# Queries, keys, features and B turned by transposing DMA reads instead of TensorE, with SyncE's reads in a fixed order

## The chip, the cores and the metric

The kernel runs on one core of one Trainium2 chip. The metric is the device time in microseconds (us) of one execution of the whole layer; lower is better. All engines of the core (TensorE, VectorE, ScalarE, GpSimd, SyncE) run beside each other and meet at semaphores. In the profile they are PE (with PEld, its weight loads), DVE, ACT, POOL and SP; a `q` behind the name means that the engine's queue waits or issues.

## The reference, cut to what matters

One layer of a decoder on 256 tokens of width 2048, all in float32:

```python
h = h + 0.5 * swiglu(rmsnorm(h, ffn1_norm), ffn1_w_gu, ffn1_w_down)          # d_ff 5632
proj = rmsnorm(h, mix_norm) @ w_in                                           # u, v, z, x, B, C, dt
a_out = chunked_sgu(gelu(u), gelu(v), gm_v_norm, gm_w_s, gm_b_s)
m_out = mamba2_group(z, xbc, dt, ...)     # conv + silu on x/B/C, chunked scan, D skip, silu(z) gate, norm
h = h + concat([a_out, m_out]) @ w_out
h = h + memory_cross_attention(rmsnorm(h, xa_norm), rmsnorm(mem, mem_norm), w_q, w_kv, w_o)  # 4 heads of 512
h = h + 0.5 * swiglu(rmsnorm(h, ffn2_norm), ffn2_w_gu, ffn2_w_down)
return rmsnorm(h, final_norm)
```

In the attention, `logits = q k^T / sqrt(512)` per head over 256 memory tokens, then a softmax, then `probs @ v` and `w_o`. The scan uses x, B and C after their convolution, with x and B needed with tokens on the partitions.

## The kernel before, in words

**Pieces of weights.** Every projection reads its weights from DRAM in pieces, mostly 1 MB into one of three `raw` buffers (`load`, line 136). ScalarE casts a piece to `hi` (line 169), VectorE subtracts to get `lo` (line 177), and TensorE multiplies the activations with both (`matmul`, line 74): products high x high, high x low and low x high. Some pieces are of kind "S", in which sums of blocks save one of eight products; the others are "C". `proj_tok`, `proj_feat` and `proj_sum` are the three shapes of a projection. A normal piece is 24 matmuls of 512 columns.

**The order of the work.** TensorE's instructions stay in program order. All others are placed by a scheduler that orders each engine's instructions when the kernel is built, unless `behind(...)` (tc.issue_after) ties one behind another. Work that belongs to an earlier stage is put off with `later(fn, by)`: `step()` counts pieces (or halves of them) and runs what is due. `by=2` therefore means "two pieces from here". Jobs that need a PSUM bank are held back while the eight banks are in use; those marked `bankless` are not.

**Activations have to be turned.** A product needs its activations with the contracted dimension on the partitions. There are two ways in this kernel. `to_operand` with a list transposes on TensorE (line 77, tile `tpose`, four 128x128 instructions for half of an operand) and splits from PSUM. `turn_over` goes through DRAM: ScalarE copies a float tile into two 16-bit halves (`halves`, line 369), GpSimd's queue writes them (`planes`, line 371), SyncE's queue reads them back with a transposing DMA (`turned`, line 375), and the split takes them from SBUF. `by=(a, b)` gives the pieces until the first read and from each read until the split. The hidden operands of both feed-forward blocks, the first two chunks of the mix operand (`xt_mix`) and the gated operand `at` are turned by DMA; the queries and keys (`qt`, `kt`, from `part` tiles), the convolved features x (`xf`, evacuated into `y` at line 854) and B (`bt`) are turned on TensorE.

**Buffers.** Temporaries share six buffers (`half_k`, tag `t2k`): halves, turned operands, partial sums (`part`), gates and others. Twelve large slots hold operands, `y`, the scan's tiles and values. SyncE's queue holds the weight reads and the transposing reads.

**Stages around the change.** After the first feed-forward block: B and C (`proj_feat`), x (`proj_feat`), V, U and Z (`proj_tok`) with the scan's steps in between (`scan_start`, `scan_decay`, `scan_apply`; `xdt` is the product of the features and dt at line 875), then `w_out`, the queries, keys, values, `w_o`, and the second feed-forward block. `attend` makes the logits of a head from `qts` and `kts`.

Of the kernel before, what the change touches and what calls it, by code (L numbers as in the profile page):

```python
# [17 lines left out]
P = 128  # L18
# [16 lines left out]
KG = 4  # L35
# [12 lines left out]
def hybrid_layer(ctx: ExitStack, tc: tile.TileContext, x, xt, mem, memt, w_gu1, w_dn1, w_in, w_s, w_out,  # L48
# [84 lines left out]
    PLAIN = {(0, 0): 0, (0, 1): 1, (1, 0): 2, (1, 1): 3}  # L133
    FOR_SUMS = {(0, 0): 0, (1, 0): 1, (1, 1): 2, (0, 1): 3}

    def load(w, r0, cs, at, fine=False):
        raw = wraw.tile([P, 2 * KP, NC], F32, name="raw")
        rows = w[r0:r0 + KP * P, :]
        if at is PLAIN and cs[1] == cs[0] + NC:
            nc.sync.dma_start(out=raw.rearrange("p (k j) n -> p k j n", j=2), in_=rows[:, cs[0]:cs[0] + 2 * NC].rearrange(  # L140
                "(k p) (j n) -> p k j n", p=P, j=2))
            return raw
        if fine:
            for (k, j), b in at.items():
                nc.sync.dma_start(out=raw[:, b, :], in_=rows[k * P:(k + 1) * P, cs[j]:cs[j] + NC])
            return raw
        for j, c in enumerate(cs):
            b, e = at[0, j], at[1, j]
            src = rows[:, c:c + NC]
            if e > b:  # L150
                nc.sync.dma_start(out=raw[:, b:e + 1:e - b, :], in_=src.rearrange("(k p) n -> p k n", p=P))
                continue
            for k, x in enumerate((b, e)):
                nc.sync.dma_start(out=raw[:, x, :], in_=src[k * P:(k + 1) * P, :])
        return raw

    def behind(instructions):

        order = ExitStack()
        for ins in instructions:  # L160
            order.enter_context(tc.issue_after(ins))
        return order

    last_cast = []

# [158 lines left out]
    def proj_feat(w, xts, n0):  # L324
        ps = {}
        n = D // P // (2 * KP)
        for i in range(n):
            raw = wraw.tile([P, 2 * KP, NC], F32, name="raw")
            nc.sync.dma_start(out=raw, in_=w[2 * i * KP * P:2 * (i + 1) * KP * P, n0:n0 + NC].rearrange(
                "(k p) n -> p k n", p=P))  # L330
            hi, lo = split(raw)
            order = [(k, c) for k in range(2 * KP) for c in range(4)]
            if i in (0, n - 1):
                order.sort(key=lambda kc: kc[1])
            for a in range(0, len(order), 4):
                for w_part in (hi, lo):
                    for k, c in order[a:a + 4]:
                        kt = 2 * i * KP + k
                        if c not in ps:
                            ps[c] = side("acc")  # L340
                        xt = xts[kt // KG][:, kt % KG, :]
                        w_kc = w_part[:, k, c * P:(c + 1) * P]
                        if w_part is hi:
                            matmul(ps[c], w_kc, xt, start=kt == 0)
                        else:
                            matmul(ps[c][:, S:], w_kc, xt[:, :S], stop=kt == D // P - 1)
            step()
        return [ps[c] for c in range(4)]
# [22 lines left out]
            nc.gpsimd.dma_start(out=planes[t * P:(t + 1) * P].rearrange("p b n -> p (b n)"), in_=halves)  # L371
        return planes

    def read_turned(to, planes, c0, n):
        nc.sync.dma_start(out=to, in_=planes[:, :, c0:c0 + n].rearrange("s b n -> (s b) n"), transpose=True)

    def turn_over(srcs, by, put):
        planes = write_planes(srcs)

        def fetch(q):  # L380
            to = half_k(F32, "turned")
            read_turned(to.bitcast(U16).rearrange("p (k s) -> p k s", k=KP), planes, q * P, KP * P)
            later(lambda: put(to.rearrange("p (k s) -> p k s", k=KP), q), by=by[1], bankless=True)

        for q in (0, 2):
            later(lambda q=q: fetch(q), by=by[0] + q / 4, bankless=True)

    def in_turn(src, last, op, c0=None):

# [66 lines left out]
    class Pieces(dict):  # L456
# [59 lines left out]
                                             op=ALU.subtract)  # L516
            return hi.ins, lo.ins

        def turn_later(self, srcs, by, c0=None, at=None):
            if at is None:  # L520
                at = self.due
                self.due += 2
            turn_over(srcs, by, lambda to, q: self.put(at + q // 2, to, q, c0))

        def later(self, srcs, c0=None, by=1):
            for q in (0, 2):
# [2 lines left out]
    class Normed:  # L529
# [8 lines left out]
        def chunk(self, n, by=1):  # L538
            srcs = [h[n][:, t, :] for t in range(NT)]
            if n < 2 and not isinstance(self.xts, Pieces):  # L540
                operand_turned(srcs, self.xts, f"xt_{self.name}{n}", self.c0 + n * KG, (2.5 + 1.5 * n, 2.5))
                self.stats(n)
            elif isinstance(self.xts, Pieces):

                for i in (2 * n, 2 * n + 1):
                    later(lambda i=i: self.xts.put(i, srcs, i % 2 * KP, self.c0 + n * KG),
                          self.bys.get(i, by))
                later(lambda: self.stats(n), self.stats_by)
            else:
                operand_later(srcs, self.xts, f"xt_{self.name}{n}", self.c0 + n * KG, by)  # L550
                self.stats(n)
# [59 lines left out]
    def ffn(nrm, w_gu, w_dn, done=None, each=None, fine=0, by_token=False):  # L611
        for c_from, c_to in ((0, 5), (5, 11)):
            kinds, turn = DN_KINDS[c_to - c_from]
            hts = Pieces(kinds, "hid", nrm.xts)
            for c in range(c_from, c_to):
                m = {}
                gs = []

                def mid(banks):
                    m["m1"], m["y"], m["z"], m["y2"] = parts_of(banks)  # L620

                def evac(t, j, ps):
                    g, u = (m["z"], m["y2"]) if t else (m["m1"], m["y"])
                    if j == 0:
                        total(g, ps, g, ALU.subtract if t else ALU.add)
                        nc.scalar.activation(g, g, AF.Silu, scale=nrm.rstd[:, t:t + 1])
                        return
                    total(u, ps, u)
                    nc.vector.scalar_tensor_tensor(out=g, in0=u, scalar=nrm.rstd[:, t:t + 1], in1=g,
                                                   op0=ALU.mult, op1=ALU.mult)  # L630
                    gs.append(g)

                if c == 0:
                    proj_sum(w_gu, 0, nrm.xts, FIRST_KINDS, (c * NC, DFF + c * NC), mid, evac, FIRST, fine)
                else:
                    proj_sum(w_gu, 0, nrm.xts, GU_KINDS, (c * NC, DFF + c * NC), mid, evac, GU_ORDER)
                hts.turn_later(gs, (1, 4))
            last = c_to == 11
            add_sum(w_dn, c_from * NC, hts, (kinds, kinds), turn, 0.5, done if last else None, each if last else None,
                    last and by_token)  # L640

# [186 lines left out]
    bt = slot([P, GROUPS, S], F32, "bt")  # L828
    ctr = slot([P, GROUPS, S], F32, "ct")
    def b_tokens(q):  # L830
        ps = side("tpose")
        for i in range(4):
            transpose(out=ps[:, i * P:(i + 1) * P], in_=bt[:, q * 4 + i, :P], identity=ident)
        nc.any.tensor_copy(out=btok[:, q * 4:q * 4 + 4, :], in_=ps.rearrange("p (g n) -> p g n", n=P))

    for c in range(4):
        xis = gather(proj_feat(w_in, nx.xts, B0 + c * NC))
# [3 lines left out]
        for i in range(4):  # L841
            conv_silu(xis[i], 16 + c * 4 + i, dst[:, (c % 2) * 4 + i, :])
        if c < 2:
            later(lambda c=c: b_tokens(c), by=2)
    y = [slot([P, HEADS, HD], F32, f"y{t}") for t in range(NT)]

    def x_tokens(c, i0, xf):
        tps = side("tpose").rearrange("p (t k s) -> p t k s", t=NT, k=2)
        for t in range(NT):
            for i in range(2):  # L850
                transpose(out=tps[:, t, i, :], in_=xf[:, i, t * P:(t + 1) * P], identity=ident)
        for t in range(NT):
            h0 = (c * 4 + i0) * 2
            nc.any.tensor_copy(out=y[t][:, h0:h0 + 4, :],
                               in_=tps[:, t].rearrange("p k (h d) -> p (k h) d", d=HD))

    for c in range(4):
        xis = gather(proj_feat(w_in, nx.xts, X0 + c * NC))
        for i0 in (0, 2):
            xf = half_k(F32, "xf").rearrange("p (k s) -> p k s", k=2)  # L860
            for i in range(2):
                conv_silu(xis[i0 + i], c * 4 + i0 + i, xf[:, i, :])
            later(lambda c=c, i0=i0, xf=xf: x_tokens(c, i0, xf), by=2 + i0 // 2)


    def per_head(ap, n):
# [5 lines left out]
    def scan_start(t, j):  # L872
        if j == 0:
            scan["xdt"] = scan[f"xdt{t}"] = xdt = slot([P, HEADS, HD], F32, "xdt")
            nc.vector.tensor_tensor(out=xdt, in0=y[t], in1=per_head(dt[:, t, :], HD), op=ALU.mult)
            nc.vector.tensor_tensor(out=y[t], in0=y[t], in1=per_head(rowb[:, 2, :], HD), op=ALU.mult)
        dec = slot([P, 16, P], F32, "dec")
        nc.gpsimd.dma_start(
# [60 lines left out]
                            base=0, channel_multiplier=-1)  # L939
    v = [slot([P, 4, NC], F32, f"v{t}") for t in range(NT)]  # L940
    ss_v = small.tile([P, NT, 4], F32, name="ss_v", bufs=1)
    for i, (by, to) in enumerate(((3, 8), (8, 12), (14, 18.5), (18.5, 23))):
        later(lambda i=i: scan_start(i // 2, i % 2), by=by)
        later(lambda i=i: scan_apply(i // 2, i % 2), by=to)
    for c in (0, 2):
# [31 lines left out]
    for c in (0, 2):  # L977
# [10 lines left out]

        proj_tok(w_in, 0, nx.xts, (U0 + c * NC, U0 + (c + 1) * NC), evac)
        for j in range(2):  # L990
            ats.turn_later(gss[j], (2.5 + 1.5 * j, 2.5))

    ss_m = small.tile([P, NT, 4], F32, name="ss_m", bufs=1)
    for c in (0, 2):
# [71 lines left out]
    def by_head(to, name, scale=None):  # L1066
        got = {}

        def take(j, t, x):
# [1 line left out]
            if scale is not None:  # L1071
                nc.scalar.mul(x, x, scale[:, t:t + 1])
            if t == 1:
                operand_later([got[j, 0], got[j, 1]], to, name, by=1 + j / 2)

        return take

# [40 lines left out]
    for hd in (0, 2):  # L1118
        heads(w_kv, mem_ts, MEM_KINDS, MEM_ORDER, hd * XD, by_head(kts, "kt", rstd_mem))
        for j in range(2):  # L1120
            later(lambda hd=hd + j: attend(hd, kts[hd]), by=2 + j / 2)

    O_KINDS = "CCCSCSCC"
    ots = Pieces(O_KINDS, "ot")
# [100 lines left out]
```

## Time and profile before

| what | value |
|---|---|
| median of 3 runs | 2428.43 us (2428.28 to 2432.98) |
| profiled execution | 2428.32 us |
| its span, first to last instruction | 2426.6 us |
| granted TensorE clock | 0.999 |
| PE / DVE / ACT / POOL busy | 2413.6 / 2033.3 / 1361.4 / 65.4 us |
| HBM read / written | 476.76 / 16.81 MB |

The busy time of an engine is summed over its instructions without overlaps, and its share is of the span. The profile lists groups of instructions by line and by tiles, written as out<-in, with the idle time of the engine just ahead of them and what ended it; the chain that ended last, which is followed back from the last instruction to whatever released it; and the instructions of each queue in order of time.

### The profile page before, as it was taken

What the parts mean: (1) busy time and instruction counts of PE and PEld (TensorE: products, weight loads), DVE (VectorE), ACT (ScalarE), POOL (GpSimd) and SP (SyncE); (2) the same over time, 40 slices, a digit from 0 to 9 for tenths busy, and PEclk for the clock granted to TensorE, in tenths of its full rate; (3) what the DMA queues carried; (4) which work ended last, traced back from release to release, by engine and by line L of the source; (5) the groups of instructions that cost most, each with busy time, mean ns of one, the idle gap of its engine ahead of it and who ended that gap; (6) DMA issues with size and microseconds to landing.
All of it is one profiled execution on the core that took longest, in us unless ns stands there. A gap on an engine that the chain in (4) does not pass through costs nothing.

```text
span 2426.6 us, 29016 instructions
## 1 busy us (share of the span) xinstructions
PE 2413.6 (99%) x11141; PEld 2010.1 (83%) x11141; DVE 2033.3 (84%) x1943; ACT 1361.4 (56%) x1261; POOL 65.4 (3%) x124
## 2 busy tenths in 40 slices
PE   9999999999999999999999999999999999999998
PEld 7888888888888888788888888888888888888886
DVE  8999889999877777655698888778899988899997
ACT  7565446555656555445555655555556644556554
POOL 1000000000000000000000000000000000000000
PEclk9999999999999999999999999999999999999999
DMA  8777667677765555567557655555567776777774
GB/s 306 234 225 232 202 208 232 220 231 231 232 196 187 181 191 175 205 194 224 190 191 244 224 191 167 176 178 174 191 217 235 225 222 197 223 229 223 233 221 151
DMA packets 264844, 510.17 MB, mean 210 GB/s; under 512 B 75760, under 2 KB 77840, under 8 KB 263936
## 3 DMA queue, kind: packets, MB, share of 16 engines
q1 hardware_dynamic: 256224, 479.00, 62.6%
q0 software_dynamic: 7648, 28.26, 3.2%
q8 instruction: 87, 1.43, 0.2%
q10 hardware_dynamic: 832, 1.05, 0.1%
q14 instruction: 53, 0.43, 0.0%
HBM read 476.76 MB, written 16.81 MB: 203 GB/s over the span
## 4 chain that ended last, share of the span: by engine, by line
PE 95%; issue 3%; ACT 1%; DVE 1%; DMA 0%; SPq 0%; POOL 0%; POOLq 0%; DVEq 0%; ACTq 0%
PE acc L74 92%; PE tpose L77 1%; PE yp L74 1%; PE o L74 0%; PE logits L74 0%; PE mixed L74 0%; DVE lo L177 0%; DMA raw<-in_w_in 0%; ACT hi L169 0%; DMA raw<-in_w_gu 0%; PE dt L74 0%; PE scores L74 0%; PE yo L74 0%; PE st L74 0%; ACT hi L191 0%
## 5 line engine op out<-in xcount | busy, mean ns | idle before, releaser
L177 DVE TENSOR_TENSOR lo<-raw,hi 128x2048 fp32r<-128x2048 f32 (+2 forms) x449 | 945.2, 2107 | 242.5 <-PE acc L74 175.4
L169 ACT CAST hi<-raw 128x2048 fp32r<-128x2048 f32 (+1 forms) x437 | 785.0, 1798 | 488.6 <-PE acc L74 418.4
L74 PE MATMUL acc<-hi,xp_ffn 128*128 128x512 f32 x1824 | 574.3, 390 | 0.0
L74 PEld LDWEIGHTS acc<-hi,xp_ffn 128*128 128x128 f32 x1824 | 342.6, 188 | 71.1
L169 ACT CAST hi<-sum 128x2048 fp32r<-128x2048 f32 x117 | 224.1, 1915 | 294.8 <-DVE sum L177 153.4
L74 PE MATMUL acc<-lo,xp_ffn 128*128 128x512 f32 x912 | 355.0, 389 | 1.3 <-DVE h L661 1.3
L177 DVE TENSOR_TENSOR lo<-sum,hi 128x2048 fp32r<-128x2048 f32 x117 | 268.1, 2292 | 37.4 <-ACT hi L169 37.4
L74 PE MATMUL acc<-hi,hid 128*128 128x512 f32 x896 | 281.3, 389 | 0.0
L74 PE MATMUL acc<-hi,xt_mix 128*128 128x512 f32 x768 | 241.5, 393 | 0.0
L74 PEld LDWEIGHTS acc<-lo,xp_ffn 128*128 128x128 f32 x912 | 171.3, 188 | 37.5 <-DVE h L661 1.7
L600 DVE TENSOR_TENSOR part<-acc,part 128x512 f32<-128x512 f32 x272 | 180.5, 686 | 23.6 <-PE acc L74 8.5
L74 PEld LDWEIGHTS acc<-hi,hid 128*128 128x128 f32 x896 | 168.1, 188 | 34.9
L74 PE MATMUL acc<-lo,hid 128*128 128x512 f32 x448 | 174.3, 389 | 0.0
L74 PEld LDWEIGHTS acc<-hi,xt_mix 128*128 128x128 f32 x768 | 144.2, 188 | 30.8 <-issue 1.0
L177 DVE TENSOR_TENSOR sum<-sum,raw 128x512 f32<-128x512 f32 x234 | 161.6, 691 | 6.2
L74 PE MATMUL acc<-lo,xt_mix 128*128 128x512 f32 x384 | 149.7, 390 | 1.1 <-DVE lo L177 1.1
L74 PE MATMUL acc<-hi,xp_ffn1s 128*128 128x512 f32 x466 | 148.5, 389 | 0.0
L74 PE MATMUL acc<-hi,xp_ffn2s 128*128 128x512 f32 x466 | 148.5, 389 | 0.0
L177 DVE TENSOR_TENSOR sum<-raw 128x1024 f32<-128x1024 f32 x117 | 142.5, 1218 | 0.0
L74 PE MATMUL acc<-xt_mix,hi 128*128 128x512 f32 x512 | 140.5, 396 | 0.0
L74 PE MATMUL acc<-hi,hids 128*128 128x512 f32 x392 | 125.2, 389 | 0.0
L74 PE MATMUL acc<-hi,memt 128*128 128x512 f32 x384 | 123.4, 392 | 0.0
(297 smaller groups left out, 3164.6 us busy)
## 6 DMA issues: line engine op xcount, KB each, us to landing
raw<-in_w_gu SPq DMA_DIRECT2D x284, 512.0 KB, 4.6
raw<-in_w_in SPq DMA_DIRECT2D x80, 1024.0 KB, 5.1
raw<-in_w_dn SPq DMA_DIRECT2D x60, 1024.0 KB, 5.2
raw<-in_w_gu SPq DMA_DIRECT2D x136, 256.0 KB, 4.9
raw<-in_w_kv SPq DMA_DIRECT2D x24, 1024.0 KB, 5.2
raw<-in_w_out SPq DMA_DIRECT2D x21, 1024.0 KB, 5.2
planes<-halves POOLq DMA_DIRECT2D x56, 256.0 KB, 4.6
raw<-in_w_dn SPq DMA_DIRECT2D x28, 512.0 KB, 4.1
```

The source lines that it names most:

```text
L74: return pe(nc.tensor.matmul(out, lhsT=lhsT, rhs=rhs, start=start, stop=stop))
L77: return pe(nc.tensor.transpose(out=out, in_=in_, identity=identity))
L169: last_cast[:] = [nc.scalar.copy(out=t[:, :n], in_=x[:, :n]).ins]
L177: last_split[:] = [nc.vector.tensor_tensor(**kw).ins]
L600: nc.vector.tensor_tensor(out=out, in0=a, in1=b, op=op)
```

## The change

- A helper `from_dram` issues SyncE's reads of weights and transposing reads. From the first down projection on (`line["kept"]`), each read issued through it is tied behind the one before it in program order. The transposing reads of the hidden operands, of the features and of B are left out of this line (`lined=False`).
- The two reads of a lined operand are one piece apart (`q / 2`) instead of half a piece.
- Chunks 0 and 1 of the mix operand and the operand `at` are read 6 and 8 pieces behind, and split one piece after each read, instead of 2.5 and 4 and 2.5 pieces.
- Queries and keys go through `operand_turned` with the same numbers, instead of the transposition on TensorE one and one and a half pieces behind.
- The features and B are written as halves at once and read by transposing DMAs straight into `y` and `btok`; no evacuation from PSUM is left.
- The logits come 9 and 11 pieces behind the keys' projection instead of 2 and 2.5. The scan's steps come 1 or 1.5 pieces later, and the product `xdt` is put into the order of the splits (`split_op`).

```diff
+    line, last_load = {"kept": False}, []
+
+    def from_dram(lined=True, **kw):
+        with behind(last_load if lined and line["kept"] else ()):
+            ins = nc.sync.dma_start(**kw).ins
+        if lined:
+            last_load[:] = [ins]
...
-    def read_turned(to, planes, c0, n):
-        nc.sync.dma_start(out=to, in_=planes[:, :, c0:c0 + n].rearrange("s b n -> (s b) n"), transpose=True)
+    def read_turned(to, planes, c0, n, lined=True):
+        from_dram(lined, out=to, in_=planes[:, :, c0:c0 + n].rearrange("s b n -> (s b) n"), transpose=True)
...
         for q in (0, 2):
-            later(lambda q=q: fetch(q), by=by[0] + q / 4, bankless=True)
+            later(lambda q=q: fetch(q), by=by[0] + (q / 2 if lined else q / 4), bankless=True)
...
-                operand_turned(srcs, self.xts, f"xt_{self.name}{n}", self.c0 + n * KG, (2.5 + 1.5 * n, 2.5))
+                operand_turned(srcs, self.xts, f"xt_{self.name}{n}", self.c0 + n * KG, (6 + 2 * n, 1))
...
-                hts.turn_later(gs, (1, 4))
+                hts.turn_later(gs, (1, 4), lined=False)
             last = c_to == 11
+            line["kept"] = True
...
     def b_tokens(q):
-        ps = side("tpose")
-        for i in range(4):
-            transpose(out=ps[:, i * P:(i + 1) * P], in_=bt[:, q * 4 + i, :P], identity=ident)
-        nc.any.tensor_copy(out=btok[:, q * 4:q * 4 + 4, :], in_=ps.rearrange("p (g n) -> p g n", n=P))
+        planes = dram.tile([P, 2, NC], U16, name="planes", tag="planes", bufs=4)
+        halves = tmp.tile([P, 2 * NC], U16, name="halves", tag="t2k")
+        halves_v = halves.rearrange("p (b g n) -> p b g n", b=2, g=4)
+        for g in range(4):
+            nc.scalar.copy(out=halves_v[:, :, g, :],
+                           in_=bt[:, q * 4 + g, :P].bitcast(U16).rearrange("p (n b) -> p b n", b=2))
+        nc.gpsimd.dma_start(out=planes.rearrange("p b n -> p (b n)"), in_=halves)
+        later(lambda: read_turned(btok[:, q * 4:q * 4 + 4, :].bitcast(U16), planes, 0, NC, False), by=1, bankless=True)
...
         if c < 2:
-            later(lambda c=c: b_tokens(c), by=2)
+            b_tokens(c)
...
     def x_tokens(c, i0, xf):
-        tps = side("tpose").rearrange("p (t k s) -> p t k s", t=NT, k=2)
-        for t in range(NT):
-            for i in range(2):
-                transpose(out=tps[:, t, i, :], in_=xf[:, i, t * P:(t + 1) * P], identity=ident)
-        for t in range(NT):
+        planes = write_planes([xf[:, i, :] for i in range(2)], S)
+
+        def fetch(t):
             h0 = (c * 4 + i0) * 2
-            nc.any.tensor_copy(out=y[t][:, h0:h0 + 4, :],
-                               in_=tps[:, t].rearrange("p k (h d) -> p (k h) d", d=HD))
+            read_turned(y[t][:, h0:h0 + 4, :].bitcast(U16).rearrange("p h d -> p (h d)"), planes, t * P, P, False)
+
+        for t in range(NT):
+            later(lambda t=t: fetch(t), by=1 + 2 * t, bankless=True)
...
-            later(lambda c=c, i0=i0, xf=xf: x_tokens(c, i0, xf), by=2 + i0 // 2)
+            x_tokens(c, i0, xf)
...
-            nc.vector.tensor_tensor(out=xdt, in0=y[t], in1=per_head(dt[:, t, :], HD), op=ALU.mult)
+            split_op(out=xdt, in0=y[t], in1=per_head(dt[:, t, :], HD), op=ALU.mult)
...
-    for i, (by, to) in enumerate(((3, 8), (8, 12), (14, 18.5), (18.5, 23))):
+    for i, (by, to) in enumerate(((4.5, 9), (9, 13), (15, 19.5), (19.5, 24))):
...
-            ats.turn_later(gss[j], (2.5 + 1.5 * j, 2.5))
+            ats.turn_later(gss[j], (6 + 2 * j, 1))
...
-                operand_later([got[j, 0], got[j, 1]], to, name, by=1 + j / 2)
+                operand_turned([got[j, 0], got[j, 1]], to, name, by=(6 + 2 * j, 1))
...
-            later(lambda hd=hd + j: attend(hd, kts[hd]), by=2 + j / 2)
+            later(lambda hd=hd + j: attend(hd, kts[hd]), by=9 + 2 * j)
```

The loads in `load` and `proj_feat` change from `nc.sync.dma_start(...)` to `from_dram(...)` and nothing else.

More of the change, by code (lines that the diff above doesn't have):

```diff
@@ L134, in hybrid_layer, with behind @@
     FOR_SUMS = {(0, 0): 0, (1, 0): 1, (1, 1): 2, (0, 1): 3}
+    def behind(instructions):
+        order = ExitStack()
+        for ins in instructions:
+            order.enter_context(tc.issue_after(ins))
+        return order
+    line, last_load = {"kept": False}, []
[4 more added lines that the diff above has]
+            last_load[:] = [ins]
     def load(w, r0, cs, at, fine=False):
@@ L139, in load @@
         if at is PLAIN and cs[1] == cs[0] + NC:
-            nc.sync.dma_start(out=raw.rearrange("p (k j) n -> p k j n", j=2), in_=rows[:, cs[0]:cs[0] + 2 * NC].rearrange(
+            from_dram(out=raw.rearrange("p (k j) n -> p k j n", j=2), in_=rows[:, cs[0]:cs[0] + 2 * NC].rearrange(
                 "(k p) (j n) -> p k j n", p=P, j=2))
@@ L144, in load @@
             for (k, j), b in at.items():
-                nc.sync.dma_start(out=raw[:, b, :], in_=rows[k * P:(k + 1) * P, cs[j]:cs[j] + NC])
+                from_dram(out=raw[:, b, :], in_=rows[k * P:(k + 1) * P, cs[j]:cs[j] + NC])
             return raw
@@ L150, in load @@
             if e > b:
-                nc.sync.dma_start(out=raw[:, b:e + 1:e - b, :], in_=src.rearrange("(k p) n -> p k n", p=P))
+                from_dram(out=raw[:, b:e + 1:e - b, :], in_=src.rearrange("(k p) n -> p k n", p=P))
                 continue
             for k, x in enumerate((b, e)):
-                nc.sync.dma_start(out=raw[:, x, :], in_=src[k * P:(k + 1) * P, :])
+                from_dram(out=raw[:, x, :], in_=src[k * P:(k + 1) * P, :])
         return raw
[L157 to L162, printed above, removed]
     last_cast = []
@@ L328, in proj_feat @@
             raw = wraw.tile([P, 2 * KP, NC], F32, name="raw")
-            nc.sync.dma_start(out=raw, in_=w[2 * i * KP * P:2 * (i + 1) * KP * P, n0:n0 + NC].rearrange(
+            from_dram(out=raw, in_=w[2 * i * KP * P:2 * (i + 1) * KP * P, n0:n0 + NC].rearrange(
                 "(k p) n -> p k n", p=P))
@@ L372, in write_planes, with turn_over @@
         return planes
-    def read_turned(to, planes, c0, n):
-        nc.sync.dma_start(out=to, in_=planes[:, :, c0:c0 + n].rearrange("s b n -> (s b) n"), transpose=True)
-    def turn_over(srcs, by, put):
+    def read_turned(to, planes, c0, n, lined=True):
+        from_dram(lined, out=to, in_=planes[:, :, c0:c0 + n].rearrange("s b n -> (s b) n"), transpose=True)
+    def turn_over(srcs, by, put, lined=True):
         planes = write_planes(srcs)
@@ L381, in fetch @@
             to = half_k(F32, "turned")
-            read_turned(to.bitcast(U16).rearrange("p (k s) -> p k s", k=KP), planes, q * P, KP * P)
+            read_turned(to.bitcast(U16).rearrange("p (k s) -> p k s", k=KP), planes, q * P, KP * P, lined)
             later(lambda: put(to.rearrange("p (k s) -> p k s", k=KP), q), by=by[1], bankless=True)
         for q in (0, 2):
-            later(lambda q=q: fetch(q), by=by[0] + q / 4, bankless=True)
+            later(lambda q=q: fetch(q), by=by[0] + (q / 2 if lined else q / 4), bankless=True)
     def in_turn(src, last, op, c0=None):
@@ L517, in sums, with turn_later @@
             return hi.ins, lo.ins
-        def turn_later(self, srcs, by, c0=None, at=None):
+        def turn_later(self, srcs, by, c0=None, at=None, lined=True):
             if at is None:
@@ L522, in turn_later @@
                 self.due += 2
-            turn_over(srcs, by, lambda to, q: self.put(at + q // 2, to, q, c0))
+            turn_over(srcs, by, lambda to, q: self.put(at + q // 2, to, q, c0), lined)
         def later(self, srcs, c0=None, by=1):
@@ L843, in hybrid_layer @@
         if c < 2:
-            later(lambda c=c: b_tokens(c), by=2)
+            b_tokens(c)
     y = [slot([P, HEADS, HD], F32, f"y{t}") for t in range(NT)]
     def x_tokens(c, i0, xf):
-        tps = side("tpose").rearrange("p (t k s) -> p t k s", t=NT, k=2)
+        planes = write_planes([xf[:, i, :] for i in range(2)], S)
+        def fetch(t):
+            h0 = (c * 4 + i0) * 2
+            read_turned(y[t][:, h0:h0 + 4, :].bitcast(U16).rearrange("p h d -> p (h d)"), planes, t * P, P, False)
         for t in range(NT):
-            for i in range(2):
-                transpose(out=tps[:, t, i, :], in_=xf[:, i, t * P:(t + 1) * P], identity=ident)
-        for t in range(NT):
-            h0 = (c * 4 + i0) * 2
-            nc.any.tensor_copy(out=y[t][:, h0:h0 + 4, :],
-                               in_=tps[:, t].rearrange("p k (h d) -> p (k h) d", d=HD))
+            later(lambda t=t: fetch(t), by=1 + 2 * t, bankless=True)
     for c in range(4):
```

## The prediction

> **What bounds the kernel now.** I read the page first, then the groups of instructions of TensorE, then the chain that ended last in order of time, then the queue of SyncE around the one place where TensorE stood still.
>
> ```profile
> span 2426.6 us, 29016 instructions
> PE 2413.6 (99%) x11141; PEld 2010.1 (83%) x11141; DVE 2033.3 (84%) x1943; ACT 1361.4 (56%) x1261; POOL 65.4 (3%) x124
> ```
>
> TensorE is busy for all but 13 us. The groups of TensorE say where it stood idle (third column), and what the transpositions are that the change takes away:
>
> ```profile
> L74 PE MATMUL acc<-lo,xp_ffn 128*128 128x512 f32 x912 | 355.0, 389 | 1.3 <-DVE h L661 1.3
> L74 PE MATMUL acc<-lo,xt_mix 128*128 128x512 f32 x384 | 149.7, 390 | 1.1 <-DVE lo L177 1.1
> L74 PE MATMUL idle<-idle 128*128 128x256 f32 x10 | 4.6, 650 | 1.3 <-DVE idle L666 1.3
> L77 PE MATMUL tpose<-ident,part 128*128 128x128 f32 x64 | 8.9, 272 | 0.0
> L77 PE MATMUL tpose<-ident,xf 128*128 128x128 f32 x32 | 4.8, 272 | 0.0
> L77 PE MATMUL tpose<-ident,bt 128*128 128x128 f32 x8 | 1.3, 280 | 0.0
> ```
>
> No other group of TensorE has idle time. Two of the three waits, 1.3 us each, are at the start (warming matmuls, first pieces), which the change does not touch; the third, 1.1 us behind a split of weights, is the only stall of the middle. So what leaves TensorE's queue shortens the kernel at full price, and what delays the weights enough to stop TensorE lengthens it.
>
> **The change part by part.**
>
> *Transpositions leave TensorE.* The queries and keys (`part`, 64), the features (`xf`, 32) and B (`bt`, 8): 104 instructions. Their price is read from the chain, in which TensorE's own work follows without a gap:
>
> ```profile
> 734.90 0.44 PE tpose L77 x4
> ...
> 759.54 0.59 PE tpose L77 x4
> ...
> 1404.30 0.87 PE tpose L77 x8
> ...
> 1546.78 0.44 PE tpose L77 x4
> ```
>
> Four take 0.44 us of the chain, eight 0.87: 0.11 us each. (These are the first, the second, an eight and the last. All others of the 104 stand there as 0.44 or 0.87 too, but for the 0.59, which includes the start behind another product; I price it as 0.44.) 104 / 4 x 0.44 = 11.4 us, all on the path. The record of one lasts 272 ns because successive records overlap.
> The Trainium skill, page "TensorE: Matmul & The Clock Gate", section "Part 4: PE-mode transpose", gives about 275 ns for one in a kernel's context. The trace's 272 ns agrees with that as a duration, but the chain's 0.11 us is what one takes from the work behind it; by the page's figure the removal would be an estimated 104 x 0.275 = 28.6 us, and the kernel would end near 2400.
>
> *The stall of 1.1 us.* SyncE's queue in time order, then the chain into the stall:
>
> ```profile
> 1059.09 11.21 SPq L375 DMA_TRANSPOSE turned<-planes  x4
> 1102.59 11.62 SPq L375 DMA_TRANSPOSE turned<-planes  x4
> ```
>
> ```profile
> 1112.36 0.51 ACT at L408
> ...
> 1112.92 1.29 SPq L375
> ...
> 1114.31 6.18 DMA raw<-in_w_in
> ...
> 1125.23 2.30 DVE lo L177
> ...
> 1127.57 4.61 PE acc L74 x19
> ```
>
> Four transposing reads in a row held SyncE for 11.62 us, since the later ones waited for buffers that ScalarE freed only with the last `at` copy; the weight read behind them started at 1114.31 and its split ended at 1127.53. The same block of 11.21 us at 1059 cost nothing. So the weights bear about 10.5 us of held queue (11.62 - 1.14), no more. The change issues these reads one piece apart (pieces 6, 7, 8, 9 behind, each used up one piece later), so no four stand together: -1.1 us. Late next is the same weight read behind one transposing read:
>
> ```profile
> L375 SPq DMA_TRANSPOSE turned<-planes x56: 1226/1290/4759, 61.3 to 2302.7; - x56
> DMA to landing us min/median/max: 3.3/4.0/8.8
> L371 POOL DMA_DIRECT2D planes<-halves x56 | 30.4, 543 | 1196.6 <-ACT halves L369 1196.6
> DMA to landing us min/median/max: 2.3/4.6/8.2
> L369 ACT COPY halves<-part 128x1024 uint16<-128x1024 uint16 x44 | 45.9, 1043 | 45.6 <-DVE part L629 45.6
> L854 ACT COPY y<-tpose 128x256 f32<-128x256 f32 x14 | 5.2, 370 | 0.8 <-DVE y L854 0.6
> ```
>
> (The first landing row is of the reads, the second of the writes.) One read holds the queue 1.29 us in the median and 4.76 at worst, both below 10.5, so cost 0.
>
> *Added, SyncE.* 16 reads for queries and keys, 16 smaller ones for the features, 2 for B: 34 x 1.29 = 44 us of queue spread over 900 us, between weight reads that wait for their buffers anyway. Cost 0 while a single read is held for less than 10.5 us; beyond that, one for one.
>
> *Added, GpSimd.* 16 + 16 + 2 = 34 writes of 0.54 us, 18 us on an engine that is 3% busy. Queued behind them are the decay and memory loads, which are due pieces later: 0.
>
> *Added, ScalarE.* 16 copies of 1.04 us (queries, keys), 16 of half that width and 8 of a quarter. For the half width the rows give between 0.37 (the 128x256 copy out of PSUM) and 1.04 us; I take 0.6, in the middle by size, and 0.37 for the quarter: 16.7 + 9.6 + 3.0 = 29 us. Away go 14 copies of 0.37, 5 us, and the evacuations of B. The cover is its idle time:
>
> ```profile
> 800.00:888.00 88.00, 88.00 (x512) 77.24 (x511) 64.43 (x89) 50.65 (x72) 0.00 (x0) 1.00 0.58 191
> 1440.00:1587.00 147.00, 147.00 (x726) 123.86 (x725) 115.84 (x118) 79.72 (x82) 0.00 (x0) 1.00 0.54 174
> ```
>
> (Columns: window, length, busy of PE, weight load, DVE, ACT, POOL, clock, DMA share, GB/s.) ScalarE has 37 us free in the first window and 67 in the second, against at most 8 and 12 added (a dozen copies of 1.04 in the second). Where four copies come together at the end of a projection, 4 x 1.04 = 4.2 us stand ahead of a cast of weights; if that is not covered it costs between 0 and 4.2 us per such place, and I take 0. DMA engines are 0.54 to 0.58 busy there; a few MB more is no bound.
>
> *Vector engine.* Operands are split from SBUF in place of PSUM at the same count; two copies of `y` go. 0.
>
> *Logits moved* from 2 and 2.5 pieces behind the keys to 9 and 11: the same matmuls, later; the keys are put at pieces 7 to 10 and so stand ready. Between 0 and a small gain or loss, as their cover for the vector engine moves to the value projection; 0. The mix operands' reads (2.5 to 6, 4 to 8) still end within the twelve pieces of the down projection: 0. Hidden operands are read as before: 0.
>
> *The scan, 1.5 pieces later,* and its first product now in the order of the splits. This is the place I trust least:
>
> ```profile
> 886.33 0.39 PE L74 MATMUL acc<-hi,xt_mix 128*128 128x512 f32 x1
> 897.22 0.51 ACT L749 ACTIVATE xf<-cacc,col 128x256 f32<-128x256 f32 x1 [2.10 <-DVE cacc L747]
> 897.63 1.89 ACT L169 CAST hi<-raw 128x2048 fp32r<-128x2048 f32 x1
> 905.64 2.29 DVE L875 TENSOR_TENSOR xdt<-y,dt 128x2048 f32<-128x2048 f32 x1
> 1044.60 65.31 PE acc L74 x288
> ```
>
> A piece of 24 matmuls takes 65.31 / 12 = 5.44 us. V starts at 886.33; the product stands after five pieces, ahead of the split of the sixth, which TensorE wants at 886.33 + 27.2 = 913.5. Two operations of 2.29 us lie between, so its input must be there at about 909. The last feature is made at 897.7; two copies (1.2 us) end at 898.9, or 900.8 behind the cast; the write lands 4.6 later, the read 4.0 after that: 907.5 to 909.4. At the slow ends (8.2 and 8.8) 917.8. So this stall lies between 0 and 8.8 us. I take 1, nearer the median landings.
>
> *Sum, from the profiled execution's 2428.32* (span 2426.6; the median of the runs shown, 2428.43, is 0.1 above it): 2428.3 - 11.4 - 1.1 + 1 = 2416.8, said as 2417.
>
> **The rivals.** A measurement of this kernel tells about 0.2% (4.9 us) from no change.
>
> *The features arrive late.* By the working above, with one of the two landings at its slow end the vector engine waits some 4 us, the splits behind it, and TensorE too: 2421. Against: medians just fit. It is still faster by over 0.2%.
>
> *The gain is given back in small waits.* Two dozen reads in order among the weights and four ScalarE copies at each projection end could each cost 0.4 us: 24 x 0.4 = 10 us, 2427, within 0.2%. For: the vector engine is 84% busy and one stall of this kind exists. Against: 56 such reads now cost one stall.
>
> *SyncE's order holds the weights.* Now a read that waits for its temporary buffer stops every weight read behind it, in program order. The mechanism is the block at 1102.59, where reads waited for ScalarE's copies. If each of the 16 reads of queries and keys is held as long as that block, it costs 16 x 1.14 = 18.2 us: 2417 + 18 = 2435, slower by over 0.2%. It decides from a hold of 10.5 us, two pieces; against it, these reads come six pieces behind the halves they read, and each fetched buffer is freed one piece later, so that two are in use at once; for it, the four partial sums of a projection's end and four halves share the same six buffers.
> The Trainium skill, page "VectorE: DVE Perf Modes", section "Rules for kernel authors", speaks against the change as well: for 128x128 use TensorE where PSUM will do as destination, and the DMA otherwise. No row here compares the two alone; the trace says only that TensorE is the full engine.
>
> *A transposition costs its whole record.* If 272 ns left the path for each, 104 x 0.272 = 28.3 us: 2428.3 - 28.3 = 2400. Against: the chain's 0.44 for four.
>
> **How the numbers follow.** Forecast (2414 to 2420, at most one or two us of new waits) 0.62; features late 0.13; given back 0.12; SyncE's order 0.11; whole records 0.02. Faster 0.62 + 0.13 + 0.02 = 0.77, within 0.2% 0.12, slower 0.11. The time is that of the first case, 2417. The range starts at 2413, below the full saving without any new wait (2415.8), and reaches to 2428, over the late features and the gain given back; it leaves out the order of SyncE and the whole records.
>
> **What would show it.** Transpositions of `part`, `xf` and `bt` gone from TensorE's groups and its busy time down by about 11 us; the 1.1 us in front of `acc<-lo,xt_mix` gone; no row of SyncE with four transposing reads in one block of 11 us outside the features; TensorE's other groups without idle time. Wrong would be: idle time of TensorE behind `lo` in the second half of the projections (order of SyncE, or ScalarE's copies), or around the sixth piece of V, with the vector engine waiting at `xdt` for a read of `planes`.

## The result: 81 us slower

The changed kernel takes 2510.19 us (median of 4 runs, 2509.23 to 2512.21), against 2428.8 for the kernel before on the same chip: a ratio of 1.0332, 95% interval 1.0314 to 1.0350. The forecast was 2417. The first lines of the page of the changed kernel, and TensorE's groups that have idle time (third column) in the middle of the kernel:

```profile
span 2507.5 us, 28974 instructions
PE 2423.8 (97%) x11037; PEld 2010.1 (80%) x11037; DVE 2032.6 (81%) x1941; ACT 1383.5 (55%) x1285; POOL 89.5 (4%) x158
L74 PE MATMUL acc<-hi,xt_mix 128*128 128x512 f32 x768 | 246.1, 399 | 18.3 <-ACT hi L177 18.3
L74 PE MATMUL acc<-lo,xt_mix 128*128 128x512 f32 x384 | 152.7, 398 | 12.3 <-DVE lo L185 12.3
L74 PE MATMUL acc<-hi,memt 128*128 128x512 f32 x384 | 128.9, 411 | 27.3 <-ACT hi L177 27.3
```

TensorE's instructions are 104 fewer, yet its busy time is 10.2 us higher (2423.8 against 2413.6), and span less busy time went from 13.0 to 83.7 us. So the span's +80.9 us is +70.7 of standing still, -11.4 of transpositions (at the prediction's 0.11 each), and, as the remainder, +21.6 of matmuls that ran slower. Most of the time that it stands still, 45.6 us, it waits for the high half of weights (`ACT hi`), which the kernel before never did in the middle: weights come late. In what follows "idle" is the third column summed over all of TensorE's groups: 3.7 us before, 75.0 in the changed kernel.

The timeline around one stall, U's projection, with the reads of `at` (SyncE's rows; a row names its start, length and count):

```profile
1070.51 0.37 SPq L147 DMA_DIRECT2D raw<-in_w_in  x1
1070.93 1.24 SPq L147 DMA_TRANSPOSE turned<-planes  x1
1075.95 0.37 SPq L147 DMA_DIRECT2D raw<-in_w_in  x1
1087.43 1.23 SPq L147 DMA_TRANSPOSE turned<-planes  x1
1088.71 0.57 SPq L147 DMA_DIRECT2D raw<-in_w_in  x1
1105.84 1.29 SPq L147 DMA_TRANSPOSE turned<-planes  x1
1107.18 3.77 SPq L147 DMA_DIRECT2D raw<-in_w_in  x3
```

The same stretch on VectorE, GpSimd and TensorE, and the clock in windows (length, busy of PE, weight load, DVE, ACT, POOL; then clock, DMA share, GB/s):

```profile
1086.72 0.69 DVE L417 TENSOR_TENSOR at<-turned,at 128x512 fp32r<-128x512 f32 x1
...
1103.49 0.54 POOL L379 DMA_DIRECT2D planes<-halves  x1 [39.07 <-ACT halves L377]
...
1100.57 0.61 PE L74 MATMUL acc<-hi,xt_mix 128*128 128x512 f32 x2
1108.28 0.79 PE L74 MATMUL acc<-hi,xt_mix 128*128 128x512 f32 x1 [7.09 <-ACT hi L177]
1110.61 0.79 PE L74 MATMUL acc<-lo,xt_mix 128*128 128x512 f32 x1 [1.53 <-DVE lo L185]
1111.20 0.63 PE L74 MATMUL acc<-hi,xt_mix 128*128 128x512 f32 x1
1111.62 0.63 PE L74 MATMUL acc<-lo,xt_mix 128*128 128x512 f32 x1
```

```profile
1094.00:1100.00 6.00, 6.00 (x28) 4.99 (x27) 1.00 (x2) 1.27 (x2) 0.00 (x0) 1.00 0.00 1
1108.30:1115.00 6.70, 5.17 (x11) 3.73 (x12) 2.85 (x2) 1.48 (x2) 0.00 (x0) 0.50 1.04 345
1115.00:1121.00 6.00, 6.00 (x27) 4.86 (x26) 5.10 (x3) 5.19 (x4) 0.00 (x0) 0.96 0.75 273
```

The third read waits until 1087.43, right behind the split that frees a temporary (it ends at 1087.41). The fourth waits until 1105.84, though its own halves had been written from 1061.03 on and landed by 1067.86. SyncE's wait ends at 1105.79, when the write of the next operand's first `halves` (issued at 1103.49) lands: it is for the temporary of these that the read waits. Each time the weight reads tied behind it wait too: none is issued between 1089.28 and 1107.18, 17.9 us, though a piece lasts 5.44. The DMA engines are empty meanwhile (share 0.00), then three pieces come at once (share 1.04). TensorE stands 7.09 and 1.53 us and goes on at half the clock (0.50, a matmul every 0.42 us in place of 0.23). The same picture stands at 1167, 1490, 1549 and 1610.

### The profile page after: what moved, and what is told of

Read it like the earlier page. It is cut to its first block, busy times and chain, and to the rows that moved or that the text cites. A ratio compares the mean times of both kernels' runs of the same rounds, so it can differ in the third digit from the quotient of the medians.

```text
span 2507.5 us, 28974 instructions
## 1 busy us (share of the span) xinstructions
PE 2423.8 (97%) x11037; PEld 2010.1 (80%) x11037; DVE 2032.6 (81%) x1941; ACT 1383.5 (55%) x1285; POOL 89.5 (4%) x158
## 4 chain that ended last, share of the span: by engine, by line
PE 43%; issue 4%; DVE 1%; DMA 1%; ACT 1%; POOL 0%; SPq 0%; POOLq 0%; DVEq 0%; ACTq 0%
PE acc L74 41%; DMA raw<-in_w_kv 1%; DVE lo L185 1%; ACT hi L177 1%; PE tpose L77 0%; PE o L74 0%; PE logits L74 0%; ACT halves L377 0%; DVE part L608 0%; DMA planes<-halves 0%; ACT part L1085 0%; DVE sum L185 0%; SPq L147 0%; ACT h L1197 0%; DVE h L1183 0%
## 5 line engine op out<-in xcount | busy, mean ns | idle before, releaser
L74 PE MATMUL acc<-hi,memt 128*128 128x512 f32 x384 | 128.9, 411 | 27.3 <-ACT hi L177 27.3
```

What stands on the lines that cost most here:

```text
L74: return pe(nc.tensor.matmul(out, lhsT=lhsT, rhs=rhs, start=start, stop=stop))
```

## The experiments

A time with an interval is a median, set against the kernel before on the same chip; a time without one is a single execution. (The kernel before had medians of 2428.4 to 2429.0 beside these runs.) In the table, "scan" tells by how many pieces the scan's first part comes later than before. In d1, d2, c3 and c1 the reads of `at` and `xt_mix` are back at the numbers of the kernel before as well; in the other rows but f1 they are late.

| run | order on SyncE | puts tied | q/k reads | scan | us | idle |
|---|---|---|---|---|---|---|
| changed kernel | kept | yes | late | +1.5 | 2510.2 | 75.0 |
| g3_order_puts_untied | kept | no | late | +1.5 | 2513.1 | 74.6 |
| e2_seven_buffers | kept | yes | late | +1.5 | 2496.7 | 62.4 |
| d1_order_kept_early | kept | yes | early | +3.5 | 2488.7 | 55.4 |
| d2_order_weights_only | weights only | yes | early | +3.5 | 2435.7 | 16.6 |
| e1_no_line | off | yes | late | +1.5 | 2474.8 | 41.5 |
| c3_qk_late_alone | off | yes | late | +3.5 | 2462.7 | 34.0 |
| c1_reads_early | off | yes | early | +3.5 | 2434.6 | 17.1 |
| t1_puts_untied | off | no | late | +1.5 | 2439.1 | 18.6 |
| t2_untied_scan_later | off | no | late | +3.5 | 2429.3 | 11.1 |
| f1_features_scan_later | off | as before | TensorE | +3.5 | 2423.7 | 4.4 |

**The order off.**

```diff
-            line["kept"] = True
```

> The changed kernel without its order: SyncE's reads are not tied to one another (line kept is never set); all else stays, the 36 new transposing reads too. Theory A (a tied read that waits for a temporary buffer or for its halves holds the weight reads behind it, and TensorE stops): of the changed kernel's 71 us of stalls in the middle only the 9.2 us at the start of the scan stays, with some 3 us of slow clock behind it, and perhaps 1 to 3 us where four reads stand together as before the change: about 2430, within 8 us. Theory B (the transposing reads themselves, by their traffic and their time on the queue, make the weights late): the stalls stay, 2490 or more.

Measured: 2474.81, ratio 1.0187 (1.0170 to 1.0204). Without the order 35.4 us are gone; 46 are left, so neither forecast held. What is left, at the end of the first query projection (SyncE, ScalarE and TensorE in the timeline of this run):

```profile
1444.74 9.43 SPq L147 DMA_TRANSPOSE turned<-planes  x3
...
1451.58 0.62 ACT L416 CAST qt<-turned 128x512 fp32r<-128x512 f32 x1 [8.19 <-DMA turned<-planes]
1452.10 0.90 ACT L422 ACTIVATE memt<-memturned,col 128x256 fp32r<-128x256 f32 x2
1452.91 1.88 ACT L177 CAST hi<-raw 128x2048 fp32r<-128x2048 f32 x1
...
1454.85 0.50 PE L74 MATMUL acc<-hi,xp_xa 128*128 128x512 f32 x1 [2.56 <-ACT hi L177]
```

A second order shows. The casts and splits of a fetched operand (`in_turn`, line 396, "puts" below) are tied into the same sequence as the weights' casts. ScalarE stood 8.19 us in front of a `qt` put whose read had come late, and the cast of weights that TensorE waited for stood behind it.

**More buffers.** Seven temporaries in place of six; to make room, the tile of the warming matmuls is halved and ten warm up in place of five.

```diff
-    tmp = ctx.enter_context(tc.tile_pool(name="tmp", bufs=6))
+    tmp = ctx.enter_context(tc.tile_pool(name="tmp", bufs=7))
```

> The changed kernel with seven shared temporaries in place of six (the room comes from the warming tile, halved; ten warming matmuls of half the width). The order stays. Theory A, with the buffers as what the reads wait for: the third read of each group no longer waits for the split of the first, so a third to two thirds of the 62 us of stalls at the operand at, the queries and the keys goes, with their slow clock: 2445 to 2485. If the reads wait for their halves and not for buffers: no change, 2505 to 2512. Theory B: no change.

Measured: 2496.73, 13.5 us less and between the two forecasts. So the temporaries are a part of what holds the reads. Even with seven, the weights are held from 1078.93 to 1103.63 by a read that leaves only behind the next operand's gates; whether buffers are all of it stays open, since a kernel without any shortage was not tried. (3.3 us of the idle time gained are in the scan's stall, 5.9 in place of 9.2.)

**The tie of the puts.** e1 with the fetched tiles of `xt_mix`, `at`, queries and keys left out of `in_turn`:

```diff
-            to = half_k(F32, "turned")
+            to = half_k(F32, "loose" if lined else "turned")
```

> The run without SyncE's order again, with one more edit: the casts and splits that turn the fetched halves of xt_mix, at, queries and keys into operands are taken out of the order that they share with the weights' casts and splits; reads stay late. Theory A with the casts as the second order: ScalarE no longer stands in a put while a cast of weights is due, the stalls shrink to those where the operand itself is wanted: 2440 to 2460 us against 2474.8 with the tie. Rival D (the tie is harmless, only the late landing of the reads counts, since the projections want these operands or their temporaries then): 2470 to 2480.

Measured: 2439.07, another 35.7 us less, just below theory A's range; idle fell from 41.5 to 18.6. The same edit on the changed kernel, with SyncE's order kept (the reads of the hidden operands stay "turned"):

> The changed kernel with SyncE's order kept as it is, and only the puts untied. The order off gave 2474.8, the order off and the puts untied 2439.1, the change 2510.2. If the two orders add: 2510.2 - 35.7 = 2474.5. If a late read held by the order makes weights late whatever ScalarE does (they are in series, the longer wait decides): 2495 to 2510, with the stalls of 7 to 9 us at 1108, 1167, 1490, 1549 and 1610 still there.

Measured: 2513.05, no gain, and 3 us above the second forecast. The two orders are in series: while SyncE holds the weights, ScalarE has nothing to cast. With the puts untied, SyncE's order costs 74.0 us (2513.05 against 2439.07), not 35.4: in the changed kernel the price of the puts hides behind it. Waits of TensorE in this run, then in the one with both orders off (us in total, times, longest):

```profile
PE acc L74 <- ACT hi L177: 45.7, 7, 10.6
PE acc L74 <- DVE lo L185: 26.4, 12, 8.4
```

```profile
PE acc L74 <- DVE lo L185: 12.5, 7, 6.0
PE tpose L77 <- DVE probs L1118: 3.2, 1, 3.2
PE idle L74 <- DVE idle L674: 1.3, 1, 1.3
```

**Late reads or the order?** Three kernels with the scan two pieces later and `at` and `xt_mix` at the numbers of the kernel before. The first has the order off and early queries and keys:

```diff
-                operand_turned([got[j, 0], got[j, 1]], to, name, by=(6 + 2 * j, 1))
+                operand_turned([got[j, 0], got[j, 1]], to, name, by=(1.5 + j, 2 + j / 2), lined=False)
```

> The changed kernel with three edits: SyncE's order is not kept; the reads of at and xt_mix go back to the pieces where the kernel before has them, and those of queries and keys are due 1.5 and 2.5 pieces behind their writes (spacing 1/4 piece) with their puts 2 and 2.5 pieces behind the reads; the scan's four parts start two pieces later still. Theory A (the six temporaries are taken by four partial sums when reads due six to nine pieces behind the writes need one, so reads come late, and weights, casts and splits stand in order behind them): all stalls of TensorE go, idle below 6 us, time 2415 to 2424. Rival B (the transposing reads of queries and keys are in themselves too much for the DMA queues, so stalls of 2 to 4 us at each group stay): idle over 20 us, 2445 or more.

Measured: 2434.60, ratio 1.0027 (1.0015 to 1.0038), idle 17.1: between the two. Then queries and keys late again:

```diff
-                operand_turned(..., by=(1.5 + j, 2 + j / 2), lined=False)
+                operand_turned(..., by=(6 + 2 * j, 1), lined=False)
```

> As the kernel with early reads, but queries and keys keep the change's numbers (reads due six and eight pieces behind the writes), with SyncE's order still not kept. Theory A: the stalls between 1450 and 1620 us that stood in the run without the order (23.3 us of its 41.5 us idle) come back and nothing else does: idle 20 to 27 us, and at the 1.41 us that each idle us cost there about 2449 us (2442 to 2456). Rival B: no different from the early reads.

Measured: 2462.71, idle 34.0. The loss returns, 7 us above theory A's range, so late reads do cost without SyncE's order. Then early reads with the order kept and all reads in it, those of `at` and `xt_mix` too (against c1; the two reads of a pair are then one piece apart instead of half a piece):

```diff
+            line["kept"] = True
...
-                operand_turned(..., by=(1.5 + j, 2 + j / 2), lined=False)
+                operand_turned(..., by=(1.5 + j, 2 + j / 2))
```

> SyncE's order kept as in the change, all reads in that order, but issued early as in the kernel with early reads (scan two pieces later too). Theory A: the order costs only what a late read makes of it; with reads early nothing is late to hold weights: 2416 to 2430, idle below 10 us. Rival C (the order itself is the fault: any read between weights ties them to ScalarE's halves and POOL's writes): stalls at each of the 20 lined pairs as in the change, 2450 or more.

Measured: 2488.73. Theory A fell: early reads in the line cost 54 us over early reads outside it. SyncE's queue in front of the first long stall with the order (first fence; GpSimd's and TensorE's rows come from the same run) and without it:

```profile
1387.50 0.37 SPq L147 DMA_DIRECT2D raw<-in_w_q  x1
1408.70 1.48 SPq L147 DMA_TRANSPOSE turned<-planes  x1
...
1406.30 0.56 POOL L379 DMA_DIRECT2D planes<-halves  x1 [1.54 <-ACT halves L377]
...
1419.03 0.79 PE L74 MATMUL acc<-hi,xp_xa 128*128 128x512 f32 x1 [8.03 <-ACT hi L177]
```

```profile
1385.38 11.80 SPq L147 DMA_DIRECT2D raw<-in_w_q  x5
1399.31 8.75 SPq L147 DMA_TRANSPOSE turned<-planes  x4
1408.15 9.76 SPq L147 DMA_DIRECT2D raw<-in_w_q  x5
```

With the order, nothing leaves SyncE for 20.8 us ahead of the read, which waits for its own source: the write of 1406.30 lands at 1408.61. Without it, weights go on meanwhile. Last, the order kept among the weights alone, with the transposing reads outside (again against c1):

```diff
+            line["kept"] = True
```

> As the kernel with the order kept and early reads (2488.7), but the transposing reads are outside the order: only the weights' reads are kept in line with one another. Theory E (what costs is a waiting read with weights tied behind it): as the early reads without the order, 2432 to 2438. Rival F (keeping the weights' own order is costly, for a scheduler moves them otherwise): 2460 or more.

Measured: 2435.65, 1.0 us over the same kernel without any order (2434.60). So what costs is a waiting read with weights tied behind it, late or early. Keeping the weights in their own order costs nothing that can be told.

**The scan.** First the edit of `xdt` alone, back out of the order of splits, with all else as changed:

```diff
-            split_op(out=xdt, in0=y[t], in1=per_head(dt[:, t, :], HD), op=ALU.mult)
+            nc.vector.tensor_tensor(out=xdt, in0=y[t], in1=per_head(dt[:, t, :], HD), op=ALU.mult)
```

> The changed kernel with the scan's first product (xdt) taken out of the order of the splits, as it was before the change; the scheduler then puts it one weight split later. If the 9.2 us at the sixth piece of V comes from that order (the vector engine waits there for the last read of the features, and the split of the sixth piece stands behind it), the stall falls by about one piece, 5.4 us, or more: 2498 to 2506. If it comes from late weights: no change, 2510.

Measured: 2505.83, just inside the first range. Its stall in V fell from 9.2 to 5.8 us, by 3.4 and not by a piece, so the order of the splits is a part of it. Then t1 with all four of the scan's parts two pieces later:

```diff
-    for i, (by, to) in enumerate(((4.5, 9), (9, 13), (15, 19.5), (19.5, 24))):
+    for i, (by, to) in enumerate(((6.5, 11), (11, 15), (17, 21.5), (21.5, 26))):
```

> The run with the order off and the puts untied (2439.1, all reads late), and the scan's four parts two pieces later. If the scan's stall (6.0 us at 916) is the last feature's late landing, it goes, with the slow clock after it: 2428 to 2432. If xdt holds the splits for another reason, the stall moves with it: 2437 to 2440.

Measured: 2429.27, 9.8 us less, no stall left in V. The rows of the changed kernel, by time:

```profile
902.88 0.51 ACT L758 ACTIVATE xf<-cacc,col 128x256 f32<-128x256 f32 x1 [1.09 <-DVE cacc L756]
...
904.34 0.54 POOL L379 DMA_DIRECT2D planes<-halves  x1 [1.71 <-ACT halves L377]
...
910.38 2.50 SPq L147 DMA_TRANSPOSE y<-planes  x2
...
915.86 2.29 DVE L185 TENSOR_TENSOR xdt<-y,dt 128x2048 f32<-128x2048 f32 x1 [10.81 <-DMA y<-planes]
918.06 2.29 DVE L185 TENSOR_TENSOR lo<-raw,hi 128x2048 fp32r<-128x2048 f32 x1
...
920.41 0.79 PE L74 MATMUL acc<-lo,xt_mix 128*128 128x512 f32 x1 [9.23 <-DVE lo L185]
```

**What the parts are worth alone.** The kernel before with only features and B turned by DMA (40 transpositions of the 104), and the scan as changed; the edit is the hunks of `b_tokens`, `x_tokens`, `xdt` and the scan's times from the diff above, and nothing else of it:

> The kernel before with one part of the change: features and B are turned by DMA, the scan's steps come later and xdt stands in the order of the splits; queries, keys, at, mix operand, logits and the order of the reads as before. 40 transpositions leave TensorE, 4.4 us. If the scan's stall of 9.2 us and its slow clock (some 3 us) come with this part alone: 2428.8 - 4.4 + 12 = 2436. If they come from the order or from the other reads: 2424.

Measured: 2433.04, ratio 1.0016 (1.0007 to 1.0026), between the two and nearer the first, with a stall of 6.3 us in V. With the scan two pieces later, by the edit shown for t2:

> The kernel before with the features and B alone turned by transposing reads (40 of the 104 transpositions, 4.4 us) and the scan's four parts two pieces later than in the change; queries, keys, at and xt_mix as before, no order on SyncE. With the scan as the change has it this part gave 2433.0, with a stall of 6.3 us at 918. If that stall and the slow clock after it are all that the part lost: idle 3 to 4 us as before, 2422 to 2426, ratio 0.997 to 0.999. If the stall only moves: 2430 to 2434.

Measured: 2423.70 (2423.12 to 2425.29), ratio 0.9976 (0.9967 to 0.9986), 5.1 us less than before and the best version found. Its page:

```profile
span 2423.5 us, 29010 instructions
PE 2410.4 (99%) x11101; PEld 2005.5 (83%) x11101; DVE 2032.0 (84%) x1941; ACT 1369.3 (56%) x1270; POOL 75.3 (3%) x142
L74 PE MATMUL acc<-lo,xt_mix 128*128 128x512 f32 x384 | 149.9, 390 | 1.3 <-DVE lo L177 1.3
```

Three more tried to get all 104, order off, puts untied and scan later: reads early as in c1,

> The kernel with early reads and the later scan, SyncE's order not kept, with one more edit: the puts of fetched halves into xt_mix, at, queries and keys leave the common order of casts and splits. Theory A (what was left of its 17.1 us idle between 1412 and 1573 us, 13 us, is ScalarE standing in a put): idle 3 to 6 us, 2417 to 2424, so faster than before by the 11.4 us of transpositions less what the clock takes. Rival (the remaining stalls are the operands' own lateness, or SyncE's reads standing before weights): 2430 to 2436, no change.

queries and keys late (`by=(6 + 2 * j, 1)`),

> Queries and keys late as in the change, all else early, scan later, SyncE's order not kept, the puts untied. Against 2462.7 us with the puts tied. Theory A (most of a late read's price comes through the tie of its put to the weights' casts): 2425 to 2435. Rival (through SyncE's queue, where a late read stands before weights even without the order): 2445 or more.

and the queries' and keys' reads and puts spread out, `by=(2.5 + 2 * j, 2)`, with `at` and `xt_mix` tied as before:

> All 104 transpositions gone; SyncE's order not kept; scan two pieces later; at and xt_mix read and put as in the kernel before; reads of queries and keys due 2.5, 3, 4.5 and 5 pieces behind their writes, their puts two pieces later and outside the order of casts. If idle falls to 5 us: 2419 to 2423, ratio 0.996 to 0.998. If stalls of 1 to 3 us at the key projections stay as in the untied runs (11 to 12 us idle): 2427 to 2431, no change.

Measured: 2430.43 (ratio 1.0007, 0.9997 to 1.0017), 2430.93, and 2426.46 (ratio 0.9989, 0.9980 to 0.9998). The first is as its rival had it, the second in theory A's range, the third between its two. Idle is 12.7, 11.6 and 11.3 us, in waits of 0.3 to 3.2 us, most of them between 1417 and 1559 us, in the query and key projections: turning those 64 gives 7 us back to TensorE and takes about as much in small waits. What each of those waits is was not taken further. The second against the first also tells what lateness costs by itself: late reads of queries and keys cost 28.1 us with the puts tied (c3 against c1) and 0.5 us with them untied.

## Why the prediction was wrong

- **Transpositions, 0.11 us each: borne out.** f1 took away 40, 4.4 us by that price, and gained 5.1 (3.4 to 8.0 by the interval). By whole records it would have been 10.9.
- **The step that failed: "Cost 0 while a single read is held for less than 10.5 us; beyond that, one for one."** I took the hold of one read from reads that the scheduler had placed freely (1.29 us median, 4.76 at worst). Tied in program order, a read waits where it was written down, for its source's write (d1) or for a temporary (the changed kernel), and the weights wait with it. SyncE's waits until a write of halves has landed (us in total, times, longest), in the kernel before, the changed kernel and d1:

```profile
SPq L375 <- DMA planes<-halves: 41.8, 28, 2.9
SPq L147 <- DMA planes<-halves: 97.5, 33, 16.5
SPq L147 <- DMA planes<-halves: 224.5, 42, 22.8
```

  At `at` the weights were held 17.9 us, 7.4 beyond 10.5, and TensorE stood 7.09 (and 1.53). That fits, but it is no rule: the 26.7 us held ahead of 1167 are 16.2 beyond, and TensorE stood 11.20 and 1.53; in d1 a hold of 25.1 us, from 1034.0 to 1059.0, brought no stall (some 10 us of the scan's matmuls stand there between those of the weights). On the changed kernel's side this term is 35.4 us, not 0, and 74.0 where the puts do not hide a part of it.
- **The rival "SyncE's order holds the weights" was the right mechanism at the wrong price and chance:** 18 us at 0.11. The argument against it, "two are in use at once", was wrong: the third read started 0.02 us after the split that freed a buffer, so it was a buffer that it waited for. That the partial sums share those buffers stood in the text and was not counted through.
- **A term that was missing: the puts in the casts' order.** The price of a late read on ScalarE was put at nothing. Once SyncE's order is off it is 35.7 us (e1 to t1); while the order is kept, nothing (g3). It was to be seen in the code alone; in the trace before no such put waits long.
- **The scan, taken at 1 with bounds 0 to 8.8: a stall of 9.23 us in the changed kernel, and 9.8 us of time from t1 to t2.** The last feature was made at 903.4 (902.88 and its 0.51), not 897.7, its write landed about 6.0 later, not 4.6, and the read about 5.4, not 4.0. Most of it is the feature's own lateness. The four copies added to ScalarE between the features stand in that stretch, but the runs do not separate them from the casts there.
- **The 1.1 us stall "goes":** it did, and 7.09 and 1.53 stand in its place.
- **Logits moved, taken at 0:** no wait for them in the changed kernel. Where weights are no longer late, TensorE waits 3.2 us (t1), 1.4 (t2) and 3.1 (g2) for `probs`, as it never did before; why was not taken further.
- **GpSimd's writes and ScalarE's copies as work:** ScalarE's busy time rose by 22.1 us, against 24 net, and GpSimd's by 24.1, against 18. Neither is a bound by its work.

By steps: 2510.2, less 35.4 (SyncE's order), less 35.7 (puts), less 9.8 (scan) is 2429.3. The first two shares hold in this order alone, for by g3 the puts taken first gain nothing. 2429.3 is the kernel before again; the 11.4 us of transpositions are used up by 7.4 us more idle (11.1 against 3.7) and, as the remainder of some 5 us, slower matmuls and what the runs don't tell apart.

## What to carry to other kernels

Before tying a transfer into the order of a queue, ask what it will wait for (its source's landing, a free buffer) and put that time against the lead of what stands behind it; durations of the same transfer placed freely did not tell it here. A tie in one queue often has a twin in another, here the operands' casts among the weights': look for both, since the removal of one shows nothing, or half, while the other holds. On a kernel whose TensorE is 99% busy, a part of a change that delays no weights (here the features, given two more pieces of room) can be worth more than all of it.

## What the runs showed of the hardware

After its longer stalls TensorE did not resume at full clock. It ran at half the clock for some 7 us (0.50 in the window from 1108.30 to 1115.00, a matmul every 0.42 us), and 0.96 in the next window. In the changed kernel slower matmuls make 21.6 us (the remainder above), a quarter of the loss, which the prediction had not priced. The Trainium skill, page "TensorE: Matmul & The Clock Gate", section "Part 1: The HAM clock gate (the "warmup" mystery)", says that the array falls to half rate after an idle window of about 3.4 us and returns after as much sustained work. The half rate agrees. The length of a single stall does not decide it here: in t2 the clock fell behind stalls of 1.07 and 1.97 us with work between, both shorter than that, while in c1 it did not fall behind one of 2.45 us at 1460. Windows behind the 1.97 of t2, and behind the 2.45 of c1:

```profile
1107.00:1112.00 5.00, 5.00 (x22) 4.15 (x23) 2.36 (x6) 2.14 (x4) 0.00 (x0) 1.00 0.92 237
1114.70:1118.30 3.60, 3.59 (x10) 2.80 (x11) 2.16 (x1) 1.03 (x1) 0.00 (x0) 0.58 0.69 207
1119.20:1130.00 10.80, 10.80 (x49) 8.97 (x48) 4.58 (x2) 3.83 (x2) 0.00 (x0) 1.00 0.55 191
```

```profile
1460.30:1466.00 5.70, 5.45 (x23) 4.06 (x24) 5.50 (x4) 4.93 (x6) 0.00 (x0) 1.00 0.58 187
```
